# Softmax sums of an attention stage: three tiles of exponentials added on GpSimd ahead of the matmul, with the work around them moved between engines

## The chip, the core and the metric

One core of a Trainium2 chip runs the whole program. The metric is the device time of one execution in microseconds. Before the change three runs took 1913.70, 1917.08 and 1929.59 us; the median, 1917.08 us, is the time that counts.

## What is computed

The reference is one step of a model of two layers over 128 prompt tokens and 1024 sample tokens. Each layer projects its input for three groups of heads (a recurrence over a matrix state, attention with eight heads, a gated linear recurrence), multiplies each group by a gate, joins them in one output projection and normalises. The change lies in the attention and in the recurrence that is woven into its slots. Cut to that:

```python
s = (einsum('bqhd,bkhd->bhqk', qn, kn) + einsum('bqhr,bkr->bhqk', qr, kr)) * SOFTMAX_SCALE
p = softmax(s, axis=-1)                  # 1024 queries x 1152 keys, 8 heads
out = einsum('bhqk,bkhd->bqhd', p, v) * silu(gm)

# one step of the recurrence (per head and direction)
sa = einsum('ebhvk,ebhk->ebhv', S, -kk_t)
S = S * w_t + sa * (kk_t * a_t) + v_t * k_t
```

The kernel computes the recurrence in chunks of 64 tokens, for which a triangular matrix of each chunk is inverted: 16x16 blocks by substitution, the rest by matmuls.

## The kernel before, in words

The attention of a layer is cut into 16 units (8 heads x 2 blocks of 512 queries), and a unit into three slots: 48 slots a layer. In a slot the function `scores` (line 1126) is called for three tiles of 128 keys; each tile takes three matmuls (rounded and remainder parts) into one of three PSUM buffers `ps_a`, and ScalarE writes the exponentials into an SBUF tile `pe` (or `mxb`) of 128 keys x 512 queries. `values` (1138) then multiplies the three tiles with the values into `ps_pv`, and `sums` (1152) adds up the exponentials over the keys: for each tile and each quarter of the queries one matmul with 32 columns of the constant `two`, into `ps_rw`. Twelve such matmuls stand in a slot. With the unit's last tile VectorE takes the reciprocal of the sums into `rl`. `finish` (1176) spreads the reciprocals by a matmul and multiplies the unit's output `o` by them on VectorE; `gate` (1186) multiplies that by the gate on GpSimd and stores it. A softmax needs row maxima: `max_q`, `max_last` and `max_rows` (1096 to 1118) find them ahead of the unit, with VectorE reducing the PSUM buffer `ps_b`.

All other work of the stage is hung into the slots. The function `at` (1230) puts a call into one of six blocks of a slot; `run` calls them. The order within a slot is A0, scores, G, A1, B, values, C, sums, S (lines 1356 to 1367). On TensorE, VectorE and ScalarE the instructions keep exactly the order in which the program is written: the wrapper `in_line` (101) ties each to the one before it on its engine. GpSimd's instructions are not tied; a scheduler at build time orders them, by when it expects their operands. DMAs of the stage are issued by SyncE.

What else the change touches:

- `split_q` (1088): the queries are split into a rounded part (ScalarE) and a remainder `qo` (GpSimd, line 1092), in block G five slots ahead of the unit.
- The recurrence runs in nine windows a layer, one in four slots, around slot c: `win_products` (823) in block B of slots c-10 and c-9, with a mask on GpSimd (844); `inv_load` (863) in C of c-9 stores and loads the triangular blocks; `inv_blocks16` (874) in C of c-8 does the substitution: 15 steps of a product (881) and a sum (882) on GpSimd over 64 partitions, each step on the one before. `inv_store` (884) in A0 of c-5 copies the result on ScalarE and VectorE, stores and reloads it by DMA, and masks `Of` on GpSimd (895). `inv_blocks` (898) in G of c-4 masks the diagonal blocks, `BdT` on VectorE and `Bd` on GpSimd (900); `inv_product` (903) follows in block B of four slots.
- In block S stand `max_rows` (one in three slots, a matmul of shape 128x4) and, in the first layer, pieces of the next layer's conditioning (`adaln_piece`, matmuls of shape 128x32).

Of the kernel before, what the change touches and what calls it, by code (L numbers as in the profile page):

```python
# [10 lines left out]
F32 = mybir.dt.float32  # L11
# [44 lines left out]
def hybrid_kernel(ctx: ExitStack, tc: tile.TileContext, x_in, cT_in, kc_in, rope_in, vec_in,  # L56
# [270 lines left out]
    for l in range(layers):  # L327
# [342 lines left out]
        sums = P("pv")  # L670
# [152 lines left out]
        def win_products(i, s):  # L823

            w = wsets[i]
            ezr, abz, abr = w["ezr"], w["abz"], w["abr"]
            bkf = w["bk"].rearrange("p d f s z t -> p d f s (z t)")
            pk, pb = P("a"), P("a")
            pkv, pbv = (t.rearrange("p (d f c) -> p d f c", d=2, f=2) for t in (pk, pb))
            for d, f in units:  # L830
                for ps, o in ((pkv, 64), (pbv, 0)):
                    for eo in range(2):
                        rhs = ezr[half_(eo), eo, d, f, s].rearrange("p z t -> p (z t)")
                        mm(ps[half_(1 - eo if o else eo), d, f, :], lhsT=bkf[half_(eo), d, f, s, o:o + 64], rhs=rhs, start=True, stop=True)
            sca_.copy(abz[:, :, :, s], pbv[:, :, :, 0:64])
            sca_.copy(abr[:, :, s], pbv[:, :, :, 64:128])
            for eo in range(2):
                K_ = half_(1 - eo)
                vtt(ezr[K_, eo, :, :, s].rearrange("p d f z t -> p d f (z t)"), pkv[K_],
                    mask[K_, :, None, :].to_broadcast([64, 2, 2, 128]), op=MUL)  # L840
            if s == 1:
                for d in range(2):
                    v_ = abr[:, d].rearrange("p s f t -> p (s f) t")
                    gtt(v_, v_, mask[:, d, None, 64:128].to_broadcast([128, 4, 64]), op=MUL)

        def win_transposes(i):
            w = wsets[i]
# [26 lines left out]
        def inv_blocks16():  # L874
            vec_.tensor_copy(flat(U_)[32:64], flat(U_)[96:128, ::-1])
            nc.gpsimd.memset(X[0:64], 0.0)
            nc.gpsimd.memset(flat(X)[0:64, ::17], 1.0)
            for t in range(15, 0, -1):
                n = 16 - t
                tv = tmp[0:64, 0:t * n].rearrange("p (a b) -> p a b", a=t)  # L880
                gtt(tv, U_[0:64, 0:t, t:t + 1].to_broadcast([64, t, n]), X[0:64, t:t + 1, t:16].to_broadcast([64, t, n]), op=MUL)  # L881
                gtt(X[0:64, 0:t, t:16], X[0:64, 0:t, t:16], tv, op=ADD)  # L882

        def inv_store(i):
# [7 lines left out]
            for eo in range(2):  # L892
                dma(Bdc[64 * eo:64 * eo + 64], X_d[:, :, :, eo].rearrange("o d a i j -> i o (d a) j"))
            for d in range(2):
                gtt(Of[:, d].rearrange("p a (b c) -> p a b c", b=4), abz[:, d].rearrange("p f s (b c) -> p (f s) b c", b=4),
                    omask[:, d, None, :, None].to_broadcast([128, 4, 4, 16]), op=MUL)

        def inv_blocks():
            for o, t_, ttt in ((1, BdT, vtt), (0, Bd, gtt)):
                ttt(t_.rearrange("p d a (b j) -> p (d a) b j", b=4), Bdc[:, o, :, None, :].to_broadcast([128, 8, 4, 16]),  # L900
                    bmask[:, None, :, None].to_broadcast([128, 8, 4, 16]), op=MUL)

        def inv_product(i, n):
# [184 lines left out]
        def split_q(u):  # L1088
            qh, qo = u["qh"], u["qo"]
            ql = qo[0:96].bitcast(F32)  # L1090
            sca_.copy(qh[0:96], ql)
            gtt(qo[0:96], ql, qh[0:96], op=SUB)
            u["mx"], u["m1"] = T("sm", [128, 16]), T("sm", [128, 16])


        def max_q(u, qt):
# [52 lines left out]
                    u["o"] = W("ep", [128, 256])  # L1149
                    act(u["o"], u["pv"][:, 0:256], AF.Copy, scale=1 / 64)  # L1150

        def sums(u):

            end = NKS // 128 - 1 if u["q0"] < NS else 0
            for j, pe in u["pe"]:
                if j == 0:
                    u["sum"] = P("rw")
                for qt in range(4):
                    mm(u["sum"][32 * qt:32 * qt + 32, 0:128], lhsT=two[:, 0:32], rhs=pe[:, 128 * qt:128 * qt + 128],
                       start=j == 0, stop=j == end)  # L1160
                if j == end:
                    u["rl"] = W("ls", [128, 128])
                    vec_.reciprocal(u["rl"], u["sum"][:, 0:128])
            u["pe"] = []

        def load_gate(u):
            h, q0 = u["h"], u["q0"]
# [69 lines left out]
        for i, u in enumerate(us):  # L1237
# [2 lines left out]
                at(s0 - 6, "C", keys, u["h"])  # L1240
            at(s0 - 6, "A0", load_q, u)
            at(s0 - 5, "G", split_q, u)
            at(s0 - 4, "A1", max_q, u, 0)
            at(s0 - 3, "A0", max_q, u, 1)
            at(s0 - 3, "A1", max_q, u, 2)
# [2 lines left out]
            at(s0 - 2, "S", max_rows, u)  # L1248
            at(s0 + 2, "G", load_gate, u)
            if s0 + 4 < nslot:  # L1250
                at(s0 + 3, "C", finish, u)
                at(s0 + 4, "G", gate, u)
        for k_, todo_ in enumerate(ada_todo[2:]):
            ada_ = adaln_piece(*todo_)
            at(5 * k_ // 2 + 1, "S", next, ada_)
# [3 lines left out]
        for i in range(9):  # L1259
# [3 lines left out]
            at(c - 9, "B", win_products, i, 1)  # L1263
            at(c - 9, "C", inv_load, i)
            at(c - 8, "B", win_transposes, i)
            at(c - 8, "C", inv_blocks16)
            at(c - 5, "A0", inv_store, i)
            at(c - 4, "G", inv_blocks)
            for n in range(4):
# [36 lines left out]

        def prompt(u):
            values(u)
            sums(u)

        ups = [dict(h=4 * g, q0=NS, i=g, pe=[]) for g in range(2)]
        for u, t_ in zip(ups, (promptq[:, 0:2], promptq[:, 2:4])):
# [7 lines left out]
        for u in ups:  # L1320
            for t_ in u["qs"]:
                nc.gpsimd.memset(t_[96:128].bitcast(F32), 0.0)
            load_q(u)
            split_q(u)
            load_gate(u)
        ada_steps()
        early(-4)
# [25 lines left out]
        todo.setdefault((0, "C"), []).insert(0, (finish, (ups[1],)))  # L1353
        at(0, "S", gate, ups[1])
        line.update(on=True, last={})
        for slot in range(nslot):
            u = us[slot // 3]
            run(slot, "A0")
            for j in range(3):
                scores(u, 3 * (slot % 3) + j)  # L1360
            run(slot, "G")
            run(slot, "A1")
            run(slot, "B")
            values(u)
            run(slot, "C")
            sums(u)
            run(slot, "S")
        line["on"] = False
        out_y = {}

# [174 lines left out]
```

## Time and profile before

| what | us |
|---|---|
| runs: lowest, median, highest | 1913.70, 1917.08, 1929.59 |
| the profiled execution's own time | 1924.55 |
| its span, first to last instruction | 1922.6 |
| attention slots of layer 0 and of layer 1, in the span | 470 to 880, 1405 to 1812 |

The profile is of one execution, and durations below come from it. PE is TensorE's matmul, PEld its weight load, DVE is VectorE, ACT is ScalarE, POOL is GpSimd and SP is SyncE. A matmul of 32-bit numbers leaves two records. Matmuls are pipelined, so a record's duration is its latency, and neighbours overlap. "128*32" is the shape of the array that a matmul uses (rows*columns). L121 and L116 are lines of helpers through which all matmuls and all VectorE and ScalarE operations go, so groups are told apart by their tiles. What stands behind "<-" in brackets is what the engine waited for; "issue" is a gap for which the profile shows no other engine.

### The profile page before, as it was taken

Reading aid. Unit: us, or ns where it says so; the run is one execution under the profiler, and the core shown is the slowest. Engines: PE = TensorE matmul, PEld = TensorE weight load, DVE = VectorE, ACT = ScalarE, POOL = GpSimd, SP = SyncE. Lnnn points to the kernel's source line nnn. Section 1 sums busy time; section 2 is a strip of 40 time slices with the busy share of each in tenths; the row PEclk is TensorE's granted clock in tenths of the full one; section 3 lists DMA queues with packets and bytes.
Section 4 is the critical chain, followed back from the end, with each engine's and each line's share of the span. In section 5 each row is a group of like instructions: output and inputs, shape, how many; then the busy total and the mean of one; then the engine's idle time right before and its main releaser. Section 6 shows DMA issues by size and latency. Waiting matters only on the chain. (4 is left out here: it accounts for less than half of the span.)

```text
span 1922.6 us, 47689 instructions
## 1 busy us (share of the span) xinstructions
PE 1801.1 (94%) x18770; PEld 1513.2 (79%) x18770; DVE 1179.4 (61%) x2512; ACT 928.9 (48%) x2108; POOL 420.9 (22%) x916
## 2 busy tenths in 40 slices
PE   5898998989999999998999989999899999999798
PEld 3898887977787777766878989998767777777587
DVE  5744454784556655766777534558755566666676
ACT  2632565763444544554126326677544454455510
POOL 0010001042344434321011100101234344342100
PEclk7999998998999999998999999998999999999999
DMA  8335444674344444437443343436632333332642
GB/s 296 110 101 161 124 129 134 220 236 122 74 108 113 109 111 106 116 110 214 160 143 120 98 151 91 117 114 209 194 85 68 91 93 89 80 89 80 208 146 88
DMA packets 328896, 250.37 MB, mean 130 GB/s; under 512 B 105112, under 2 KB 268512, under 8 KB 327648
## 3 DMA queue, kind: packets, MB, share of 16 engines
q1 hardware_dynamic: 328672, 247.32, 43.6%
q8 instruction: 148, 2.42, 0.5%
q14 instruction: 76, 0.62, 0.1%
HBM read 168.55 MB, written 78.64 MB: 129 GB/s over the span
## 5 line engine op out<-in xcount | busy, mean ns | idle before, releaser
L121 PE MATMUL ps_a<-t,t 128*128 128x384 f32 (+4 forms) x6096 | 713.6, 296 | 35.8 <-ACT pe L116 13.8
L121 PEld LDWEIGHTS ps_a<-t,t 128*128 128x128 f32 (+1 forms) x6096 | 653.8, 167 | 70.9 <-ACT pe L116 21.9
L116 DVE TENSOR_REDUCE sm<-ps_b 128x1 f32<-128x1024 f32 (+1 forms) x164 | 179.8, 1096 | 124.7 <-PE ps_b L121 124.1
L116 ACT ACTIVATE pe<-ps_a 128x512 f32<-128x512 f32 (+1 forms) x296 | 168.5, 576 | 168.0 <-PE ps_a L121 155.4
L121 PE MATMUL ps_a<-q,t 128*128 128x512 f32 x864 | 223.5, 403 | 5.3 <-DVE ep L116 5.3
L121 PEld LDWEIGHTS ps_a<-q,t 128*128 128x128 f32 x864 | 161.4, 190 | 49.8 <-issue 7.3
L121 PE MATMUL ps_a<-t,q 128*128 128x512 f32 (+1 forms) x544 | 160.6, 379 | 0.0
L116 DVE TENSOR_TENSOR t<-kp,t 128x512 fp32r<-128x512 f32 (+2 forms) x128 | 83.2, 677 | 94.9 <-ACT t L116 85.5
L157 POOL TENSOR_TENSOR sm<-sm,nhalf 128x1 f32<-128x1 f32 (+1 forms) x54 | 40.5, 751 | 410.2 <-DVE sm L116 408.4
L121 PE MATMUL ps_pv<-pe,t 128*64 128x256 f32 x928 | 125.1, 391 | 0.0
L121 PE MATMUL ps_b<-t,q 96*128 96x512 f32 (+1 forms) x384 | 109.0, 378 | 13.5 <-DVE sm L116 8.4
L121 PE MATMUL ps_a<-t,kp 128*128 128x512 f32 (+1 forms) x304 | 116.3, 382 | 0.0
L121 PEld LDWEIGHTS ps_a<-t,q 128*128 128x128 f32 x544 | 99.8, 188 | 19.3
L116 ACT CAST t<-kp 128x512 fp32r<-128x512 f32 (+2 forms) x128 | 71.9, 602 | 86.9 <-DMA kp<-in_wft_dram 39.2
L121 PEld LDWEIGHTS ps_b<-t,q 96*128 96x128 f32 x384 | 63.1, 193 | 36.8 <-DVE sm L116 11.5
L121 PEld LDWEIGHTS ps_pv<-pe,t 128*64 128x64 f32 x928 | 60.0, 138 | 34.6 <-issue 8.0
L881 POOL TENSOR_TENSOR t<-t 64x15 f32<-64x15 f32 (+2 forms) x270 | 71.7, 265 | 62.1 <-DVE t L116 25.4
L882 POOL TENSOR_TENSOR t<-t 64x15 f32<-64x15 f32 (+2 forms) x270 | 73.1, 271 | 20.4
L116 DVE TENSOR_TENSOR t<-ps_a,t 128x512 f32<-128x512 f32 (+2 forms) x106 | 65.5, 625 | 17.5 <-ACT t L116 10.1
L121 PE MATMUL ps_rw<-pe,two 128*32 128x128 f32 x1888 | 75.7, 277 | 0.0
L121 PEld LDWEIGHTS ps_cx<-t,t 128*64 128x64 f32 (+1 forms) x1752 | 64.5, 138 | 13.9 <-issue 5.7
L116 ACT CAST q<-pe 128x512 fp32r<-128x512 f32 x32 | 19.9, 621 | 113.9 <-PE ps_a L121 102.0
(261 smaller groups left out, 2940.9 us busy)
## 6 DMA issues: line engine op xcount, KB each, us to landing
kp<-in_wft_dram SPq DMA_DIRECT2D x64, 256.0 KB
kp<-in_wmod_dram SPq DMA_DIRECT2D x64, 256.0 KB
rw<-in_x_dram SPq DMA_DIRECT2D x36, 256.0 KB
gate_d<-pe SPq DMA_DIRECT2D x48, 192.0 KB
bk_d<-ls SPq DMA_DIRECT2D x36, 256.0 KB
zr_d<-abz SPq DMA_DIRECT2D x36, 256.0 KB
t<-bk_d SPq DMA_DIRECT2D x18, 512.0 KB
t<-v_d SPq DMA_DIRECT2D x144, 64.0 KB
```

Of the source, the lines that this page charges most:

```text
L116: return lambda *a, **k: in_line(getattr(self.eng, op)(*a, **k))
L121: return in_line(nc.tensor.matmul(*a, **k))
L157: gtt(out, t[:, :n], nhalf.to_broadcast([128, n]), op=POW)
L881: gtt(tv, U_[0:64, 0:t, t:t + 1].to_broadcast([64, t, n]), X[0:64, t:t + 1, t:16].to_broadcast([64, t, n]), op=MUL)
L882: gtt(X[0:64, 0:t, t:16], X[0:64, 0:t, t:16], tv, op=ADD)
```

## The change

The three tiles of a slot are added up on GpSimd (`add_exps`) as their exponentials come, and four matmuls in place of twelve sum the result over the keys. They are issued one slot later, between block B and the values. The reciprocal becomes a function of its own (`invert`), after block C of the slot behind the unit's last one, and its result lies in `w2`, a tile of weights that is no longer needed there; `finish` and `gate` move one slot back. The remainder of the queries (`split_low`, block C), the mask of `win_products`, `Of` and `Bd` go from GpSimd to VectorE. The substitution becomes a generator of 16 pieces, spread over the blocks from C of slot c-8 to B of slot c-6.

```diff
-                    gtt(v_, v_, mask[:, d, None, 64:128].to_broadcast([128, 4, 64]), op=MUL)
+                    vtt(v_, v_, mask[:, d, None, 64:128].to_broadcast([128, 4, 64]), op=MUL)
...
             for t in range(15, 0, -1):
+                yield
                 n = 16 - t
...
-                gtt(Of[:, d].rearrange("p a (b c) -> p a b c", b=4), abz[:, d].rearrange("p f s (b c) -> p (f s) b c", b=4),
+                vtt(Of[:, d].rearrange("p a (b c) -> p a b c", b=4), abz[:, d].rearrange("p f s (b c) -> p (f s) b c", b=4),
...
-            for o, t_, ttt in ((1, BdT, vtt), (0, Bd, gtt)):
-                ttt(t_.rearrange("p d a (b j) -> p (d a) b j", b=4), Bdc[:, o, :, None, :].to_broadcast([128, 8, 4, 16]),
+            for o, t_ in ((1, BdT), (0, Bd)):
+                vtt(t_.rearrange("p d a (b j) -> p (d a) b j", b=4), Bdc[:, o, :, None, :].to_broadcast([128, 8, 4, 16]),
...
-            gtt(qo[0:96], ql, qh[0:96], op=SUB)
             u["mx"], u["m1"] = T("sm", [128, 16]), T("sm", [128, 16])
+
+        def split_low(u):
+            qo = u["qo"]
+            vtt(qo[0:96], qo[0:96].bitcast(F32), u["qh"][0:96], op=SUB)
...
-        def sums(u):
+        def sums(u, pe, first, last_):
             end = NKS // 128 - 1 if u["q0"] < NS else 0
-            for j, pe in u["pe"]:
-                if j == 0:
-                    u["sum"] = P("rw")
-                for qt in range(4):
-                    mm(u["sum"][32 * qt:32 * qt + 32, 0:128], lhsT=two[:, 0:32], rhs=pe[:, 128 * qt:128 * qt + 128],
-                       start=j == 0, stop=j == end)
-                if j == end:
-                    u["rl"] = W("ls", [128, 128])
-                    vec_.reciprocal(u["rl"], u["sum"][:, 0:128])
-            u["pe"] = []
+            if first == 0:
+                u["sum"] = P("rw")
+            for qt in range(4):
+                mm(u["sum"][32 * qt:32 * qt + 32, 0:128], lhsT=two[:, 0:32], rhs=pe[:, 128 * qt:128 * qt + 128],
+                   start=first == 0, stop=last_ == end)
+
+        def invert(u):
+            u["rl"] = w2[:, u["i"] % 2, 0:128]
+            vec_.reciprocal(u["rl"], u["sum"][:, 0:128])
+
+        def add_exps(u, n):
+            if n == 1:
+                u["acc"] = W("ls", [128, 512])
+                gtt(u["acc"], u["pe"][0][1], u["pe"][1][1], op=ADD)
+            else:
+                gtt(u["acc"], u["acc"], u["pe"][2][1], op=ADD)
...
+            at(s0 - 5, "C", split_low, u)
...
-                at(s0 + 3, "C", finish, u)
-                at(s0 + 4, "G", gate, u)
+                at(s0 + 4, "C", finish, u)
+                at(s0 + 5, "G", gate, u)
...
-            at(c - 8, "C", inv_blocks16)
+            sub_ = inv_blocks16()
+            for k_ in range(16):
+                k6 = 6 * (c - 8) + 4 + 3 * k_ // 4
+                at(k6 // 6, ("A0", "G", "A1", "B", "C", "S")[k6 % 6], next, sub_, None)
...
+        behind = None
         for slot in range(nslot):
             u = us[slot // 3]
             run(slot, "A0")
             for j in range(3):
                 scores(u, 3 * (slot % 3) + j)
+                if j:
+                    add_exps(u, j)
             run(slot, "G")
             run(slot, "A1")
             run(slot, "B")
+            if behind:
+                sums(*behind)
             values(u)
             run(slot, "C")
-            sums(u)
+            if slot % 3 == 0 and behind:
+                invert(behind[0])
+            behind = u, u.pop("acc"), u["pe"][0][0], u["pe"][-1][0]
+            u["pe"] = []
             run(slot, "S")
+        sums(*behind)
+        invert(us[-1])
```

## Rows read from the trace of the kernel before

**Rows 1.** Busy time by stage: us, busy (instructions) of each engine, clock, DMA share, GB/s.

```profile
core 0: us, PE busy (x) PEld busy (x) DVE busy (x) ACT busy (x) POOL busy (x), PEclk, DMA share, GB/s
...
470.00:880.00 410.00, 400.97 (x6489) 308.54 (x6488) 250.22 (x519) 204.04 (x451) 152.12 (x364) 0.98 0.42 111
...
1405.00:1812.00 407.00, 392.76 (x6254) 300.08 (x6252) 251.65 (x498) 208.56 (x460) 151.42 (x357) 0.99 0.38 97
```

**Rows 2.** Waits of weight loads, 470 to 880 us: total us, times, longest.

```profile
PEld ps_b L121 <- DVE sm L116: 4.8, 5, 3.4
...
PEld ps_pv L121 <- ACT pe L116: 1.8, 5, 0.7
```

**Rows 3.** Records with the tile `two`: count, ns least/median/most, first and last start.

```profile
L121 PE MATMUL ps_rw<-pe,two x1888: 272/273/423, 459.6 to 1805.8; 128*32 128x128 f32 x189
...
L121 PE MATMUL ps_rw<-mxb,two x448: 272/273/298, 490.4 to 1800.5; 128*32 128x128 f32 x150
```

**Rows 4.** Weight loads in time, 470 to 486 us: start, us, what, [idle before].

```profile
474.50 0.20 PEld L121 LDWEIGHTS ps_rw<-pe,two 128*32 128x32 f32 x8 [0.33 <-issue]
...
481.96 0.13 PEld L121 LDWEIGHTS ps_a<-ckvh,kp 128*64 128x64 f32 x1 [0.17 <-issue]
...
483.68 0.59 PEld L121 LDWEIGHTS ps_rw<-pe,two 128*32 128x32 f32 x24 [0.30 <-issue]
484.47 0.30 PEld L121 LDWEIGHTS ps_b<-t,q 96*128 96x128 f32 x2 [0.20 <-issue]
```

**Rows 5.** Weight loads in time, 538 to 550 us.

```profile
539.12 0.59 PEld L121 LDWEIGHTS ps_rw<-pe,two 128*32 128x32 f32 x24
539.72 0.20 PEld L121 LDWEIGHTS ps_b<-kc,sm 128*4 128x4 f32 x2
```

**Rows 6.** GpSimd's groups, 470 to 880 us: count, busy us, mean ns, idle before.

```profile
L1092 POOL TENSOR_TENSOR q<-q,q 96x512 fp32r<-96x512 f32 x14 | 17.8, 1269 | 27.9 <-ACT q L116 19.4 <-DVE modT L116 8.5
...
L844 POOL TENSOR_TENSOR t<-t,kc 128x256 f32<-128x256 f32 x16 | 11.4, 729 | 2.9 <-ACT t L116 2.9
L900 POOL TENSOR_TENSOR t<-t,kc 128x512 f32<-128x512 f32 x9 | 10.8, 1199 | 41.1 <-DMA t<-X_d 30.8 <-DVE rs L116 6.2 <-DVE ep L116 4.0
```

**Rows 7.** GpSimd in time, 608 to 630 us, one substitution from end to end.

```profile
614.80 0.73 POOL L1189 TENSOR_TENSOR ep<-ep,ep 128x256 f32<-128x256 f32 x1 [6.00 <-DVE ep L116]
616.27 0.21 POOL L881 TENSOR_TENSOR t<-t 64x15 f32<-64x15 f32 x1 [0.73 <-POOL ep L1189]
...
628.45 0.21 POOL L882 TENSOR_TENSOR t<-t 64x15 f32<-64x15 f32 x1
```

**Rows 8.** All engines in time, 629 to 642 us.

```profile
631.14 1.02 ACT L116 COPY t<-t 32x256 f32<-32x256 f32 x2
633.53 0.60 ACT L116 ACTIVATE mxb<-ps_a 128x512 f32<-128x512 f32 x1 [1.37 <-PE ps_a L121]
...
635.31 0.54 PEld L121 LDWEIGHTS ps_a<-t,t 64*64 64x64 f32 x16 [0.36 <-issue]
```

**Rows 9.** All engines in time, 518.9 to 523 us.

```profile
519.04 0.21 POOL L882 TENSOR_TENSOR t<-t 64x15 f32<-64x15 f32 x1
...
520.19 1.04 ACT L116 COPY t<-t 32x256 f32<-32x256 f32 x2
521.91 0.60 ACT L116 ACTIVATE pe<-ps_a 128x512 f32<-128x512 f32 x1 [0.68 <-PE ps_a L121]
```

**Rows 10.** VectorE's groups, whole run: count, busy us, mean ns, idle before.

```profile
L116 DVE TENSOR_TENSOR kp<-pe,q 128x512 fp32r<-128x512 f32 x32 | 22.5, 703 | 8.1 <-PE ps_a L121 6.1 <-ACT q L116 1.9
...
L116 DVE TENSOR_TENSOR st<-st,wcs 128x256 f32<-128x256 f32 x36 | 16.3, 454 | 1.2
...
L116 DVE TENSOR_TENSOR t<-t,kc 128x512 f32<-128x512 f32 x18 | 13.5, 749 | 8.3 <-DMA t<-X_d 8.3
```

**Rows 11.** All engines in time, 789 to 793 us.

```profile
789.84 1.52 POOL L900 TENSOR_TENSOR t<-t,kc 128x512 f32<-128x512 f32 x1 [4.06 <-DMA t<-X_d]
790.38 1.26 DVE L116 TENSOR_TENSOR rw<-rw,rw 128x256 f32<-128x256 f32 x1
```

More of the change, by code (lines that the diff above doesn't have):

```diff
@@ L1308, in prompt @@
             values(u)
-            sums(u)
+            sums(u, u["pe"][0][1], 0, 0)
+            invert(u)
+            u["pe"] = []
         ups = [dict(h=4 * g, q0=NS, i=g, pe=[]) for g in range(2)]
@@ L1324, in hybrid_kernel @@
             split_q(u)
+            split_low(u)
             load_gate(u)
@@ L1363, in hybrid_kernel @@
             run(slot, "B")
+            if behind:
+                sums(*behind)
             values(u)
             run(slot, "C")
-            sums(u)
+            if slot % 3 == 0 and behind:
+                invert(behind[0])
+            behind = u, u.pop("acc"), u["pe"][0][0], u["pe"][-1][0]
+            u["pe"] = []
             run(slot, "S")
+        sums(*behind)
+        invert(us[-1])
         line["on"] = False
```

## The prediction

> **What bounds the kernel now.** I read the busy time by stage first, then who waits for whom in the attention stage, then the order of TensorE's weight loads, and last GpSimd. The change touches only the attention slots, 48 a layer, which fill 470 to 880 us and 1405 to 1812 us: about 8.5 us a slot. There TensorE is busy 401 of 410 us and 393 of 407, VectorE 250, ScalarE 204 to 209, GpSimd 152 [rows 1]; the clock is granted almost in full. TensorE's queue hardly waits for another engine: its weight loads stood 4.8 us in the whole first stage for VectorE's row maxima and 1.8 us for an exponential [rows 2]. So a record taken from TensorE here shortens the slot, and time added elsewhere costs only where TensorE comes to wait for it.
>
> **TensorE: fewer sums.** Each of a slot's 12 sums matmuls leaves two records; the run has 1888 + 448 = 2336 of them [rows 3], which is 2 x (96 slots x 12 + 16 of the prompt). Adding the three tiles first leaves 4 matmuls, 8 records. What is one worth? Not the 0.27 us that each lasts, since four column groups run side by side. The weight loads tell: a group of 8 takes 0.20 us, a group of 24 takes 0.59 [rows 4], so 16 records cost 0.39 us. 96 slots x 0.39 = 37.4 us, the main term. From above: two thirds of everything between the group's start at 483.68 and the next load at 484.47, 0.53 us a slot or 51 us; from below nothing, if another engine becomes late.
>
> **TensorE: the sums at another place.** They stood between block C and block S; now they stand between B and the values. A change of the array's shape leaves gaps: 0.20 us from the sums' 128x32 to 96x128, 0.17 from 32x64 to 128x64 [rows 4]. Most slots swap one such change for another: taken as nothing, with 0.2 us either way. But in some 45 of the 96 slots block S holds work of the same or a like narrow shape (30 times the maxima's transposition, 16 times the conditioning matmuls), which today follows the sums with no gap: loads end at 539.71, the next starts at 539.72 [rows 5]. There the sums now need a change of their own, about 0.2 us: +9 us, bounds 0 and +19. The Trainium skill speaks against the move as well: "TensorEngine Tiling (Array Packing)", section Tiling Modes, Key Properties, says that a change of tiling mode, not of tile, drains the engine. The gaps of [rows 4] agree with that.
>
> In return the values, which wait for the third exponential, have the sums in front of them, and the sums' operand is a slot old: of the 1.8 us a layer waited there [rows 2] I take back 2 us in both layers.
>
> **GpSimd.** It gets two additions of 128x512 a slot. The trace shows none; the nearest is the split's subtraction of 96x512 with two full operands, 1.27 us [rows 6]. I take 1.27 (bounds 1.2, the masked 512 columns there with a broadcast operand, and 1.5). 96 additions a layer are 122 us; the split, the masks and the diagonal blocks leave (17.8 + 11.4 + 10.8 = 40 us [rows 6], plus the off-diagonal mask). GpSimd goes from 152 to about 230 of 400 us: enough room on average. An addition ends a few us behind its exponential, and its sum is due in block B of the next slot, 8 us on, so the new wait should cost TensorE nothing; if it does, the values and all that follows on TensorE stand behind it (rival four). The exponentials' buffers now also wait for the additions, with several us to spare.
>
> The tight place is the substitution. Behind its result stand, in program order, ScalarE's and VectorE's copies in block A0 three slots later, and behind those on ScalarE the exponentials of that slot. Today it runs from 616.27 to 628.66 [rows 7]; ScalarE's copies take 1.02 us and the next exponential starts at 633.53 [rows 8], so the result could come until 632.5, 3.9 us later, without harm. In a tight case the result comes at 519.25, copies at 520.19, the exponential at 521.91 [rows 9]: 1.6 us to spare. Now four additions (5.1 us) and, in two of three cases, a gate of 0.73 us fall into this stretch, and a split of 1.27 us leaves it: about 4.5 us later. Reading all 18 windows in this way, seven have under 5 us to spare, the others up to 10. TensorE itself can bear about 1 us more: the exponential of 633.53 ends at 634.13 and block B, which needs its buffer, begins at 635.31 [rows 8]. So seven windows lose on average some 0.9 us: +6 us, bounds 0 and 18 x 2 = 36 us. Spreading the substitution itself removes no instruction; it lets the additions in between. I price it at nothing else.
>
> **VectorE.** A window hands it four products of 128x256 at 0.454 us and one of 128x512 at 0.749; each of 18 groups of queries in a layer, one subtraction of 96x512, 0.703 at most [rows 10]. 9 x (4 x 0.454 + 0.749) + 18 x 0.703 = 36 us a layer: 250 becomes 286 of some 400 us. It waits mostly for TensorE, so this hides, at the price of a few longer waits for row maxima: +3 us, bounds 0 and +10. The subtraction now waits on VectorE for ScalarE's copy of the block before; with chain and maxima queued behind it, that copy must not be late, and its operand was loaded a slot earlier.
>
> **VectorE against GpSimd.** At 789.84 GpSimd's masked product takes 1.52 us, and VectorE's 128x256 addition behind it at 790.38 takes 1.26 instead of about 0.45 [rows 10, 11]: the two hold each other up. In the +3 above stand some 3 such VectorE operations a slot, a third of which meet an addition and lose about 0.4 us, all beside TensorE. "SBUF — State Buffer", section "SBUF: two separate sides", of the Trainium skill states this as a rule: a VectorE operation with two SBUF inputs and a GpSimd operation that reads SBUF exclude each other, and the later one fully blocks. By it rival two, below, would come; the trace agrees in the row shown.
>
> The finish and the gate come one slot later and the reciprocal follows the next slot's block C: nothing waits for them but the store of a head's output, which is read after the stage; at the stage's end the last addition hides behind the last values, within 1 us. DMAs are the same in number; the gate's two stores move past the loads of one slot on SyncE's queue, which has room.
>
> **The sum.** -37.4 + 9 - 2 + 6 + 3 = -21.4 us. The profiled execution took 1924.55 us, so 1903.1. The runs' median is 1917.08, 7.5 us below it: 1895.7, said as 1896.
>
> **Rivals.** *One: GpSimd's lateness eats the gain.* If every window's substitution is 2 us late for TensorE, 36 us go in place of the 6 I took: -21.4 + 30 = +8.6, about 1926; at half of it -21.4 + 12 = -9.4, 1908. Either is no change that can be measured. For it: 12.4 us of substitution and four additions in two slots of 8.2. Against: the other two slots of a window are light.
> *Two, the slower side: the shared access makes VectorE the bound.* Should each of its three two-input operations a slot be blocked as at 790.38, by 0.8 us, VectorE needs (250 + 36) / 48 = 6.0 plus 2.4 = 8.4 us a slot. It decides from the point where VectorE's slot passes TensorE's 8.1; with its in-order waits for TensorE on top, say 8.8 us, the slots cost 96 x 0.3 = 29 us more than today: 1946. Against: GpSimd's subtractions of 1.27 us keep a mean of 1.269 [rows 6], so clashes are rare.
> *Three: more comes back.* The full 0.53 us a slot and no dearer changes of shape: -51 + 6 = -45, 1872.
> *Four: the sums wait for the addition after all,* if GpSimd's queue puts it behind other work by over a slot: 0.3 us a slot gives 29 us back, 1925, no change.
>
> **How the numbers follow.** A measurement of this kernel tells about 1% from no change, 19 us. My forecast has 0.48, centred on 1896, with its own range 1884 to 1908: 0.39 of it faster by over 1%, 0.09 within. Rival one 0.24 (0.21 within, 0.03 slower), two 0.11 (0.09 slower, 0.02 within), three 0.10 (faster), four 0.07 (0.06 within, 0.01 slower). Faster 0.49, the same 0.38, slower 0.13. The range goes from just above rival three to the near edge of rivals one and four: 1874 to 1922.
>
> **What would show it.** Right: 800 records of the sums instead of 2336; groups of 8 at 0.20 us; both stages shorter by some 10 us, slots near 8.3 us; additions near 1.27 us, GpSimd busy about 230 us a stage; no waits of TensorE for GpSimd. Wrong: weight loads for the sums released by GpSimd (rival four); ScalarE's copies of the substitution waiting for GpSimd in most windows (one); VectorE's SBUF products at twice their time, with row maxima late (two); gaps of 0.3 us and more on both sides of the sums (the second term mis-sized).

## The result, and the profile after

The changed kernel is slower: 1949.17 us median (1939.02 to 1951.89) beside 1921.31 us (1913.70 to 1929.59) of the kernel before in the same session, ratio 1.0134 [1.0106, 1.0161]. The forecast was 1896, its range ended at 1922. The profiled execution took 1951.04 us, its span 1949.2.

The busy time of the two attention stages, which answers to [rows 1] (us, busy time and instructions of each engine, granted clock, DMA share, GB/s):

```profile
470.00:880.00 410.00, 387.38 (x5695) 285.62 (x5694) 290.18 (x565) 197.35 (x439) 225.34 (x404) 0.97 0.41 105
...
1405.00:1812.00 407.00, 376.60 (x5374) 277.19 (x5369) 275.33 (x518) 193.47 (x436) 219.72 (x407) 0.96 0.33 83
```

TensorE does less and is less busy, 387 of 410 us in place of 401; VectorE (290) and GpSimd (225) have what the forecast gave them (286 and 230). Nobody is full, and yet the same work no longer fits: from the first score of slot 0 to that of slot 47, layer 0 takes 409.6 us in place of 402.7, layer 1 412.8 in place of 390.5. The clock fell with TensorE's pauses: 0.97 for 0.98 and 0.96 for 0.99, which is 4 + 12 us of full-speed time.

The sums' records (count, ns least/median/most, first and last start) answer to [rows 3], the weight loads in time to [rows 4]:

```profile
L121 PE MATMUL ps_rw<-ls,two x768: 269/297/423, 489.6 to 1835.7; 128*32 128x128 f32 x192
...
L121 PE MATMUL ps_rw<-pe,two x32: 272/359/423, 461.1 to 1415.3; 128*32 128x128 f32 x32
```

```profile
543.11 0.16 PEld L121 LDWEIGHTS ps_rw<-ls,two 128*32 128x32 f32 x8
543.47 0.20 PEld L121 LDWEIGHTS ps_pv<-mxb,t 128*64 128x64 f32 x4 [0.20 <-issue]
```

So the change does what it says: 800 records for 2336, a group of 8 in 0.16 us, a 0.20 us gap for the change of shape behind it.

What TensorE waits for: weight loads, 470 to 885 us, beside [rows 2], and then matmuls, 1405 to 1840 us (total us, times, longest):

```profile
PEld ps_b L121 <- DVE sm L116: 12.2, 14, 3.5
...
PEld ps_a L121 <- DVE ys L116: 7.9, 4, 2.8
...
PEld ps_rw L121 <- POOL ls L1173: 2.2, 4, 1.7
```

```profile
PE ps_b L121 <- DVE sm L116: 9.2, 10, 3.2
PE ps_a L121 <- DVE ys L116: 8.8, 4, 2.6
PE ps_a L121 <- DMA t<-zr_d: 7.7, 4, 3.4
```

The wait for VectorE's row maxima was 4.8 us and is 12.2. That for VectorE's addition to `ys` is 7.9; before the change, in the same stretch, it was

```profile
PEld ps_a L121 <- DVE ys L116: 0.9, 2, 0.5
```

Four waits of 2.2 us in all are for an addition: the sums hardly wait for GpSimd. In layer 1 there is a third kind, for the window's loads.

How VectorE comes to be late is seen in slot 10 of layer 0 (all engines in time; start, us, engine, operation, [idle before]):

```profile
557.50 1.27 POOL L1173 TENSOR_TENSOR ls<-pe,pe 128x512 f32<-128x512 f32 x1 [2.27 <-ACT pe L116]
557.54 1.77 DVE L116 COPY t<-t 32x256 f32<-32x256 f32 x2
...
559.34 1.90 DVE L116 TENSOR_TENSOR t<-abz,kc 128x256 f32<-128x256 f32 x2
...
559.70 1.25 POOL L1175 TENSOR_TENSOR ls<-ls,pe 128x512 f32<-128x512 f32 x1
...
561.95 0.41 DVE L116 TENSOR_TENSOR ys<-ps_a,ys 128x256 f32<-128x256 f32 x1
...
562.42 1.50 PE L121 MATMUL ps_a<-t,t 64*64 64x128 f32 x28 [2.60 <-DVE ys L116]
```

Two copies take 1.77 us (0.69 before), because one of them ends only after the addition of 557.50 has; two products, work moved to VectorE, take 1.90 (0.84 alone), because one ends only after the addition of 559.70 has. Behind them on VectorE stands the addition to `ys` that frees TensorE's PSUM buffer, and TensorE stands 2.60 us for it. Before the change these matmuls waited for nothing, and the slot took 8.6 us; now it takes 13.8.

### The profile page after: what moved, and what is told of

Its sections match the earlier page's. It is cut to its first block, busy times and chain, and to the rows that moved or that the text cites. A ratio compares the mean times of both kernels' runs of the same rounds, so it can differ in the third digit from the quotient of the medians.

```text
span 1949.2 us, 44758 instructions
## 1 busy us (share of the span) xinstructions
PE 1787.8 (92%) x17234; PEld 1474.2 (76%) x17234; DVE 1268.7 (65%) x2638; ACT 926.9 (48%) x2108; POOL 557.6 (29%) x982
## 5 line engine op out<-in xcount | busy, mean ns | idle before, releaser
L121 PE MATMUL ps_a<-t,t 128*128 128x384 f32 (+4 forms) x6096 | 717.7, 298 | 67.7 <-DVE ys L116 15.8
L121 PE MATMUL ps_a<-q,t 128*128 128x512 f32 x864 | 229.8, 409 | 9.1 <-ACT pe L116 6.7
L121 PE MATMUL ps_pv<-pe,t 128*64 128x256 f32 x928 | 130.8, 405 | 0.0
L1173 POOL TENSOR_TENSOR ls<-pe,pe 128x512 f32<-128x512 f32 x58 | 76.1, 1313 | 116.7 <-ACT pe L116 113.9
L1175 POOL TENSOR_TENSOR ls<-ls,pe 128x512 f32<-128x512 f32 x78 | 100.3, 1285 | 3.4 <-ACT pe L116 0.7
L883 POOL TENSOR_TENSOR t<-t 64x15 f32<-64x15 f32 (+2 forms) x270 | 75.3, 279 | 18.6
```

The costliest lines, as they stand in the source:

```text
L121: return in_line(nc.tensor.matmul(*a, **k))
L1173: gtt(u["acc"], u["pe"][0][1], u["pe"][1][1], op=ADD)
L1175: gtt(u["acc"], u["acc"], u["pe"][2][1], op=ADD)
```

## The experiments

Theory one: GpSimd's additions and VectorE's SBUF operations hold each other up, and VectorE, which works in order, frees TensorE's buffers late. Theory two: the additions make GpSimd late, and what stands behind GpSimd (the copies of the substitution, the gate's store on SyncE's queue) makes TensorE late. In the first four expectations theory three lays the loss to the work moved to VectorE, and theory four to the sums' new place. "Slot lengths" below run from a slot's first score to the next slot's.

**e1_no_adds: the changed kernel without additions.**

```
-                u["acc"] = W("ls", [128, 512])
-                gtt(u["acc"], u["pe"][0][1], u["pe"][1][1], op=ADD)
-            else:
-                gtt(u["acc"], u["acc"], u["pe"][2][1], op=ADD)
+                u["acc"] = val(0)
```

> The changed kernel without the additions on GpSimd: the four sums matmuls of a slot read a tile of values that is long finished, so the softmax is divided by something else. Theory 1 (the additions and VectorE's operations on SBUF shut each other out, TensorE then waits for VectorE, and the clock halves behind such waits): all of that goes, ratio to the kernel before 0.983 to 0.990, about 1890 to 1902 us. Theory 2 (GpSimd's queue is too full, so the substitution's result and the gate's store come late): the same ratio, as that queue empties too. Theory 3 (the work moved to VectorE is too much for it by itself): the loss stays, ratio 1.005 or more, 1930 us or more. Theory 4 (the sums at their new place cost TensorE what they save): 0.997 to 1.003.

1896.80 us, ratio 0.9846 [0.9800, 0.9893]. The additions alone cost what lies between this and 1949: 52 us. All else in the change together gains 28 us. Theories one and two had forecast the same here, so this run does not tell them apart; the causes that theories three and four name do not explain the loss.

**e2_sums_alone: in addition the four moved operations back on GpSimd and the substitution in one piece.** The diff is that of e1 and the change's own, reversed.

> As the run without additions, and besides masks, off-diagonal and diagonal blocks and the low part back on GpSimd and the substitution in one piece: only the 4 matmuls a slot later are left of the change (on a finished tile, so the softmax is divided by something else). Theories 1, 2 and 3: ratio 0.980 to 0.990, my main term of 37 us less some 10 for changes of shape. Theory 4: 0.997 to 1.003. Against the run without additions it tells what the moved work costs where no addition stands in its way: theory 1 within 0.004, theory 3 at least 0.015 below.

1910.12 us, ratio 0.9907 [0.9874, 0.9939]: the four matmuls a slot later are worth 15 us by the medians and 18 by the ratio, less than the 30 of the first three terms of the sum. The moved work and the spread substitution, which e1 has and this run has not, are worth 13 us more: where no addition stands in its way the moved work gains. Two rows of the weight loads' waits tell part of what the 30 us lacked, 470 to 885 us, and below them the second one before the change:

```profile
PEld ps_b L121 <- DVE sm L116: 10.6, 14, 3.0
...
PEld ps_pv L121 <- issue: 9.7, 48, 0.4
```

```profile
PEld ps_pv L121 <- issue: 3.7, 19, 0.4
```

TensorE, now earlier, meets VectorE's row maxima more often: 14 waits of 10.6 us for 5 of 4.8 [rows 2], and 12.1 us for 8.4 in layer 1, 9.5 us in both. And the gap for the change of shape stands before the values of every slot (48 times, 9.7 us, where it was 19 times, 3.7). All gaps of that kind, on all tiles, grow by 7.4 us in layer 0 and, without its longest one, 6.7 in layer 1. Besides, slot 29 of layer 1 is 6.6 us longer than before, for a reason that e6 shows.

**e3_adds_vector: the changed kernel with additions on VectorE, and the other parts undone as in e2.**

```
-                gtt(u["acc"], u["pe"][0][1], u["pe"][1][1], op=ADD)
+                vtt(u["acc"], u["pe"][0][1], u["pe"][1][1], op=ADD)
-                gtt(u["acc"], u["acc"], u["pe"][2][1], op=ADD)
+                vtt(u["acc"], u["acc"], u["pe"][2][1], op=ADD)
```

> The two additions of a slot on VectorE instead of GpSimd; masks, blocks, low part and the substitution in one piece back on GpSimd as before. VectorE gets 96 x 0.69 = 66 us a stage more, GpSimd nothing. Theory 1: no additions hold GpSimd's side of the access, so most of the gain appears, ratio 0.985 to 0.997. Theory 2: the same, GpSimd's queue is as before. Theory 3 (VectorE has no room in the stage): slower, ratio 1.01 or more. Theory 4: 1.00 or more.

2014.92 us, ratio 1.0458 [1.0406, 1.0510]: far off for theories one and two, on the side of theory three (1.01 or more). TensorE's waits, 1405 to 1840 us:

```profile
PE ps_a L121 <- DVE t L116: 13.3, 9, 1.9
PE ps_a L121 <- DVE ys L116: 12.8, 8, 2.0
PE ps_b L121 <- DVE sm L116: 11.0, 11, 3.5
```

VectorE, busy 282 of 407 us, has no room for them: what counts is what stands in front of the operation that frees a buffer, not the sum of busy time. This is theory one's second half, shown without any addition on GpSimd.

**e4_moves_only: the kernel before, with masks, blocks, products and low parts on VectorE.**

```
-                gtt(v_, v_, mask[:, d, None, 64:128] ... op=MUL)
+                vtt(v_, v_, mask[:, d, None, 64:128] ... op=MUL)
...
-            gtt(qo[0:96], ql, qh[0:96], op=SUB)
...
+            at(s0 - 5, "C", split_low, u)
```

> The kernel before with nothing but the mask, the off-diagonal and diagonal blocks and the low part moved to VectorE (36 us a stage). Theories 1, 2 and 4: within 0.995 to 1.004. Theory 3: ratio 1.015 or more, for then the moved work alone makes the loss.

1912.01 us, ratio 0.9935 [0.9910, 0.9960]: better than both kernels, and just under the 0.995 at which the expectation of theories one, two and four ended. The forecast had put +3 us on this part. Where its slots gain is narrow: slot 12 of each layer, 13.2 to 10.3 us and 16.1 to 10.9, where the kernel before waits for row maxima and loses its clock (0.80 from 1505 to 1522 us); the other slots keep their length within 0.7 us, but for slot 0 of layer 0 (-1.6) and slot 44 of layer 1 (+2.3).

**e5_fill: in place of each addition one of 8 columns and two fills, together about as long, that read hardly anything.**

```
-                gtt(u["acc"], u["acc"], u["pe"][2][1], op=ADD)
+                gtt(u["acc"][:, 0:8], u["acc"][:, 0:8], u["pe"][2][1][:, 0:8], op=ADD)
+            for _ in range(2):
+                nc.gpsimd.memset(u["acc"][:, 8:512], 0.25)
```

and likewise for the first addition of a slot.

> The changed kernel, with GpSimd's additions cut to 8 columns (they wait for the same exponentials) and, behind each, two fills of the other 504 columns of the same array: GpSimd is kept busy at the same points, about as long, and reads hardly anything from SBUF. The sums over keys are those of the fill. Theory one, the additions lengthen VectorE's operations through SBUF (in the changed kernel the sum of two halves in the group norm takes 0.69 us in the mean against 0.42 without additions, the window's second product 0.73 against 0.42): with little read, that is gone, near the run without additions, 1895 to 1910 us, ratio 0.984 to 0.992, and these two operations near 0.42 us. Theory two, the additions make what stands behind them on GpSimd late (the substitution, the gate's product and its store on SyncE's queue): no difference from the changed kernel, 1940 to 1955 us, ratio 1.008 to 1.016.

1905.25 us, ratio 0.9889 [0.9846, 0.9932]. The stages of this run, and then VectorE's groups in it and in the changed kernel (whole run; count, busy us, mean ns, idle before; the group of `rw` mixes shapes in both):

```profile
470.00:880.00 410.00, 392.66 (x5780) 288.32 (x5779) 279.12 (x588) 207.58 (x461) 222.34 (x602) 0.98 0.44 116
1405.00:1812.00 407.00, 384.27 (x5480) 283.78 (x5479) 277.78 (x564) 207.62 (x459) 215.19 (x579) 0.98 0.39 100
```

```profile
L116 DVE TENSOR_TENSOR rw<-rw,rw 128x256 f32<-128x256 f32 (+2 forms) x56 | 24.8, 442 | 14.4 <-ACT rw L116 14.1
...
L116 DVE TENSOR_TENSOR t<-abz,kc 128x256 f32<-128x256 f32 x36 | 13.7, 423 | 0.6
...
L116 DVE TENSOR_TENSOR sm<-sm 128x4 f32<-128x4 f32 x32 | 5.4, 170 | 1.1
L116 DVE TENSOR_SCALAR smr<-gmv 128x4 f32<-128x4 f32 x18 | 4.8, 268 | 0.6
```

```profile
L116 DVE TENSOR_TENSOR rw<-rw,rw 128x256 f32<-128x256 f32 (+2 forms) x56 | 33.8, 604 | 14.7 <-ACT rw L116 14.5
L116 DVE TENSOR_TENSOR t<-abz,kc 128x256 f32<-128x256 f32 x36 | 24.9, 732 | 0.6
...
L116 DVE TENSOR_SCALAR smr<-gmv 128x4 f32<-128x4 f32 x18 | 10.5, 581 | 0.6
L116 DVE TENSOR_TENSOR sm<-sm 128x4 f32<-128x4 f32 x32 | 9.8, 307 | 1.1
```

GpSimd is as busy as in the changed kernel (222 and 215 us for 225 and 220), if not quite as late: a substitution takes 12.7 us in the mean from its first operation to its last, 14.6 in the changed kernel, 10.9 in e1. VectorE's products and additions are back at their length (25 window products that met a fill took 0.422 us in the mean), and 44 of the 52 us are back with them. TensorE's waits for VectorE in the slots fall from 39.8 us to 18.4, about as in e1 (table behind the experiments). This settles the greater part for theory one. Of the remaining 8 us, to e1, 5.6 stand in one slot, 34 of layer 0:

```profile
771.31 1.03 ACT L116 COPY t<-t 32x256 f32<-32x256 f32 x2 [6.38 <-POOL t L883]
773.02 0.09 PEld L121 LDWEIGHTS ps_a<-ep,kc 128*2 128x2 f32 x2 [3.61 <-ACT pe L116]
```

ScalarE's copies wait for the substitution there, and TensorE for an exponential behind them: GpSimd's lateness by itself. The two runs' intervals overlap.

**e6_gate_vector: the changed kernel with the gate's product on VectorE.**

```
-            gtt(gm, gm, u["o"], op=MUL)
+            vtt(gm, gm, u["o"], op=MUL)
```

> The changed kernel, with the gate's product on VectorE instead of GpSimd, nothing else. Theory two: the gate's stores no longer wait on SyncE's queue behind GpSimd's additions, the window's loads behind them come in time, and the two slots of layer 1 that are 6.8 and 6.4 us longer than before lose that: 1930 to 1940 us, ratio 1.003 to 1.009. Theory one: 1945 to 1952 us, ratio 1.011 to 1.016, one more VectorE operation for each third slot and nothing else.

1944.82 us, ratio 1.0090 [1.0061, 1.0120], between the two forecasts and hardly apart from the changed kernel's. But the two slots named are back: slots 17 and 29 of layer 1, 15.0 and 14.6 us in the changed kernel for 8.2 before, are 8.1 again. In the profiled execution the slots of both layers are 19 us shorter than in the changed kernel, but the stretch between the two layers' slots is 10 us longer. That stretch takes 526 to 539 us in the profiled executions, so a few us between totals say little of the slots. What happens in the two slots named is seen in slot 17 of the changed kernel (GpSimd, SyncE's queue, then TensorE):

```profile
1557.54 0.74 POOL L1200 TENSOR_TENSOR ep<-ep,ep 128x256 f32<-128x256 f32 x1
```

```profile
1553.45 0.38 SPq L994 DMA_DIRECT2D yr_d<-ys  x1
1558.30 1.24 SPq L1204 DMA_DIRECT2D yT_d<-ep  x2
1559.63 1.28 SPq L816 DMA_DIRECT2D t<-zr_d  x2
```

```profile
1563.44 0.66 PE L121 MATMUL ps_a<-t,t 64*64 64x128 f32 x2 [3.38 <-DMA t<-zr_d]
```

The gate's store (L1204) waits on SyncE's queue for GpSimd's late gate (L1200), and the window's loads (L816) behind it come 3.4 us late for TensorE. It does not need the additions: in e1, e2 and e5 slot 29 of layer 1 is 6.1, 6.6 and 5.9 us longer than before too. TensorE's clock then fell; the stretch around it (granted clock in the third column from the right):

```profile
1530.00:1563.00 33.00, 29.19 (x492) 22.44 (x490) 22.50 (x47) 17.58 (x41) 19.89 (x42) 1.00 0.36 90
1563.00:1570.00 7.00, 6.12 (x62) 3.91 (x64) 1.38 (x2) 0.75 (x3) 2.03 (x2) 0.51 0.28 70
1570.00:1600.00 30.00, 26.96 (x428) 19.80 (x426) 23.04 (x38) 14.10 (x31) 12.49 (x21) 1.00 0.26 63
```

After a pause of 3.4 us TensorE works some 7 us at 1.2 instead of 2.4 GHz: the wait costs about as much again.

**e7_one_piece: the changed kernel with the substitution unspread.**

```
-                k6 = 6 * (c - 8) + 4 + 3 * k_ // 4
+                k6 = 6 * (c - 8) + 4
```

> The changed kernel, with the substitution in one piece again, as before. Theory one: it costs little by itself, 1945 to 1955 us, ratio 1.010 to 1.017. Theory two: a run of about 10 us on GpSimd ahead of the next slot's additions makes the sums wait, TensorE stands, 1955 to 1975 us, ratio 1.017 to 1.027; against that, the substitution ends a slot earlier, and if its end is what is late for the copies on VectorE and ScalarE, 1925 to 1940 us, ratio 1.000 to 1.009.

1949.91 us, ratio 1.0117 [1.0068, 1.0166]: as theory one said. These runs tell no cost and no gain of the spreading.

**e8_half_slots: additions in slots 0 and 3 of each four only.**

```
-                if j:
+                if j and slot % 4 in (0, 3):
                     add_exps(u, j)
...
-            behind = u, u.pop("acc"), u["pe"][0][0], u["pe"][-1][0]
+            if "acc" in u:
+                behind = u, u.pop("acc"), u["pe"][0][0], u["pe"][-1][0]
+            else:
+                behind = None
+                for j, pe in u["pe"]:
+                    sums(u, pe, j, j)
+                if slot % 3 == 2:
+                    invert(u)
```

> The changed kernel, with additions and late sums only in slots 0 and 3 of each four; in slots 1 and 2 the three tiles' sums are taken from the exponentials in the same slot, 12 matmuls, as before. The slots that the change lengthened most are 2 of each four (18.7 us in each layer) and 1 of layer 1 (8.4 us). Theory one (clash in the slots where VectorE's operations of the window stand): these 46 us go and 48 slots give back 8 records of 24 ns each, 9 us: 1905 to 1918 us, ratio 0.990 to 0.997. Theory two (lateness, which gathers in slots 3 and 0 where the substitution runs): half the additions stand beside the substitution as before, half the loss stays: 1922 to 1940 us, ratio 0.999 to 1.009.

1939.45 us, ratio 1.0083 [1.0058, 1.0108]: a miss for theory one as put. The expectation gave 9 us for the sums of the 48 slots; but 8 matmuls more in a slot are 16 records, so it is 768 records, and at the 24.6 ns of [rows 4] (0.59 us for 24) 19 us. TensorE's waits, 470 to 885 us, name a wait that the edit itself brought, the reciprocal that still reads the one PSUM buffer of the sums:

```profile
PE ps_rw L121 <- DVE w L116: 10.1, 4, 4.0
```

**e12_half_early: the same with the reciprocal ahead of the values.**

```
                 sums(*behind)
+                if slot % 3 == 0:
+                    invert(behind[0])
             values(u)
             run(slot, "C")
-            if slot % 3 == 0 and behind:
-                invert(behind[0])
```

> The run with additions in slots 0 and 3 of each four, with one edit: the reciprocal of the finished sums comes right behind the last late sums, ahead of the values, instead of after the values. In the run before, 20.7 us of TensorE's waits (10.1 and 10.6 us in the two stages, 4 each) were for that reciprocal: the next sums were written to the same PSUM buffer in the same slot. Theory one: these waits go, the time comes where the first expectation had put it: 1915 to 1926 us, ratio 0.995 to 1.000. Rival (half of the additions still hold VectorE up half as much, and the waits only change their name): 1932 to 1940 us, ratio 1.004 to 1.008.

1926.82 us, ratio 1.0019 [1.0002, 1.0035], one us above theory one's range, which would end 10 us higher with 19 us for the sums (the run has 1568 records of them, the changed kernel 800). e1 plus 19 us is 1916, so the additions that are left cost some 11 us. In each stage TensorE still waits once for the reciprocal, which the edit brought; the row reads the same in both:

```profile
PE ps_rw L121 <- DVE w L116: 3.6, 1, 3.6
```

In slots 2 of each four, which have no additions here, TensorE's matmuls wait 3.6 us in both layers together: 4.4 before the change, 32.7 in the changed kernel. So most of the loss was gathered there, as the expectation of e8 had it, and additions in slots 0 and 3 cost little.

**e9_adds_alone: the changed kernel with masks, blocks, products and low parts back on GpSimd and the substitution in one piece; the additions stay.** The diff is the change's own, reversed, but for additions and sums.

> The changed kernel with its three other parts undone: masks, blocks and low parts on GpSimd again where they were, substitution in one piece; additions on GpSimd and the late sums stay. Theory one: of the 52 us by which VectorE's operations beside additions are longer in the changed kernel, 11.1 are the window's second product, 1.7 the low parts of q and about half of 3.4 the blocks, so some 14 us of 52 are no longer VectorE's; that share of the 53 us that the additions cost comes back, about 15 us, against which GpSimd has 45 us a stage more in front of its additions and late work: 1935 to 1946 us, ratio 1.005 to 1.011. Rival: what counts is how late GpSimd runs, and 45 us more a stage make it worse: 1955 to 1975 us, ratio 1.016 to 1.027.

1942.77 us, ratio 1.0081 [1.0049, 1.0114], in theory one's range, but only in part by its reason. TensorE's waits for VectorE are 10 us less than in the changed kernel; those for ScalarE, behind a substitution that now takes 16.5 us, are 7 us more; and slots 17 and 29 of layer 1, where the window's loads came late, are 13 us shorter together. Beside e2 the additions cost 33 us here, beside e1 they cost 52. Of this difference (25 us in the slots' lengths) 14 lie in the same two slots, so that additions are dearer the more VectorE has to do through SBUF is shown for 11 us at most.

**e10_c5_aside: the changed kernel with the copies of the inverse on ScalarE and the window's two products on GpSimd.**

```
-            vec_.tensor_copy(flat(XO)[32:64], flat(X)[32:64, ::-1])
+            sca_.copy(flat(XO)[32:64], flat(X)[32:64, ::-1])
...
-                vtt(Of[:, d].rearrange( ...
+                gtt(Of[:, d].rearrange( ...
```

> The changed kernel, with the four VectorE operations of the window's slot c-5 taken off VectorE: the two copies of the inverse on ScalarE, the two products of the window on GpSimd. Theory one, in its narrow form: these stand in line ahead of the addition that frees TensorE's buffer in that slot, and of the 18.7 us that the slots 2 of each four are longer in each layer nearly all goes: 1918 to 1932 us, ratio 0.997 to 1.004. Theory one, in its wide form, any lengthened operation of VectorE makes the next buffer late, wherever it stands: these four carry 15 of 52 us, so 15 of 53 come back: 1931 to 1940 us, ratio 1.004 to 1.008. Rival: the slots are long because of GpSimd's work itself; with two more operations there, 1950 to 1960 us, ratio 1.013 to 1.018.

1934.29 us, ratio 1.0046 [1.0023, 1.0070]: in the range of the wide form, but not for its reason. Slots 17 and 29 of layer 1 are 14 us shorter together than in the changed kernel, because the wait for the window's loads is gone; the slots of both layers together are 11 us shorter. Slots 2 of each four are as long as in the changed kernel (19 and 21 us more than before), and what TensorE waits for there has changed. Its waits for VectorE's `ys`, 15.8 us in the changed kernel, are gone, as the narrow form had it; those for exponentials are 26.0 us for 8.0. Slot 34 of layer 0:

```profile
780.30 2.07 ACT L116 COPY t<-t 32x256 f32<-32x256 f32 x4 [5.33 <-POOL t L883]
782.39 1.08 ACT L116 ACTIVATE pe<-ps_a 128x512 f32<-128x512 f32 x2
783.04 0.09 PEld L121 LDWEIGHTS ps_a<-ep,kc 128*2 128x2 f32 x2 [2.61 <-ACT pe L116]
```

Four copies on ScalarE wait for the substitution, the exponentials behind them, and TensorE for these: rival one of the prediction, met here.

**e11_one_operand: the fills of e5 as operations with one operand.**

```
-                nc.gpsimd.memset(u["acc"][:, 8:512], 0.25)
+                nc.gpsimd.tensor_scalar(u["acc"][:, 8:512], u["pe"][j][1][:, 8:512], 1.0, None, op0=ADD)
```

> As the run with fills, but each fill is an operation that reads one operand, the exponentials of one tile, and adds 1 (504 columns); again two behind each addition of 8 columns, and the sums over keys are those of such an array. If VectorE is held up only beside operations with two operands from SBUF: as the run with fills, 1898 to 1910 us, ratio 0.986 to 0.992. If any reading holds it up: as the changed kernel, 1938 to 1955 us, ratio 1.007 to 1.016. In proportion to what is read, in between.

2082.51 us, ratio 1.0817 [1.0783, 1.0852], outside every forecast, and so no answer by its time: the operation lasts 1.48 us where two operands took 1.27. GpSimd's group, 470 to 885 us:

```profile
L1177 POOL TENSOR_SCALAR ls<-pe 128x504 f32<-128x504 f32 x128 | 189.7, 1483 | 24.9 <-ACT pe L116 22.9
```

GpSimd is then busy 339 of 415 us, and the exponentials wait for their buffers. VectorE's operations give part of an answer. Those that met nothing but this operation lengthen, but less than beside an addition: the masks of diagonal blocks, 128x512, take 0.88 us in the mean of 19 and at most 1.10 (0.68 alone; at most 1.77 beside an addition), products of 128x256 0.46 in the mean of 30 and at most 0.82 (0.41 alone). The run also shows lateness as a cost of its own, at some 6 us of added work a slot; at 2.5 us (e5) there was little of it.

**TensorE's waits in the slots, by run.** The table sums the idle time before TensorE's matmuls from slot 0 to slot 47 of both layers, by the engine that ended it, in one profiled execution each. "Clock" is the time that the granted clock lacked to full speed there, "slots" the length of both stretches (all in us).

| run | VectorE | ScalarE | DMA | clock | slots |
|---|---|---|---|---|---|
| before | 15.3 | 1.1 | 1.0 | 6.8 | 793 |
| changed kernel | 39.8 | 9.7 | 7.7 | 25.5 | 822 |
| e1, no additions | 18.6 | 1.5 | 4.8 | 5.1 | 769 |
| e5, fills | 18.4 | 5.8 | 4.6 | 11.9 | 778 |
| e9, additions alone | 29.9 | 16.4 | 0.6 | 13.7 | 801 |
| e10, c-5 aside | 24.1 | 28.5 | 0.1 | 21.5 | 812 |
| e12, half, early | 21.3 | 3.4 | 0.5 | 6.8 | 789 |

## Why the prediction was wrong

**What held.** The records, the gap, the additions' duration (1.27 to 1.33 us), both engines' busy time, and that the sums would not wait for GpSimd (rival four) came as said. 50 of 94 slots are shorter, most of them by 0.2 to 1.1 us.

**The step that failed: "VectorE against GpSimd".** The size of the clash was in the text: 3 operations a slot, a third of them meeting an addition, 0.4 us each, which is 38 us in 96 slots. Over both stages of the changed kernel 106 VectorE operations beside an addition are, in sum, 52 us longer than the median of the same operation without one: about 0.5 us each. (That this sum is as large as what the additions cost is chance: TensorE loses what stands behind such an operation, and the clock besides.) What was wrong are the words "all beside TensorE", and with them the +3 us. VectorE works in order, and behind a held operation stands, soon, one that TensorE waits for: a row maximum, or an addition that frees a buffer. e5 gives 44 us for this term in place of 3; in the slots, by the table, they are 21 us of waits for VectorE, 4 for ScalarE, 3 for loads, and 14 that the lower clock cost. That GpSimd's subtractions kept a mean of 1.269 in the kernel before was no evidence: it is VectorE's operations that lengthen, and the additions are many more.

**Rival two** had this mechanism and a near time, 1946, at 0.11, but the wrong point from which it decides. It asked when VectorE's sum of work passes TensorE's slot; VectorE is at 290 of 410 us and no bound. In-order waits decide, long before that point. e3 shows the same without GpSimd: additions on VectorE cost 105 us beside e2 at a busy time that would have fitted. The Trainium skill's rule in "SBUF — State Buffer", section "SBUF: two separate sides", that the later of the two is blocked for the whole instruction, was quoted and then priced at a third. The runs agree with it for the window's product: beside an addition the window's product rises from 0.424 to at most 1.569 us, that is by 1.15, nearly the whole 1.27; beside fills, which read nothing, it stays at 0.423.

**Smaller steps.** The saved matmuls and their new place, -37.4 + 9 - 2 = -30 us, measured -15 by the medians, -18 by the ratio (e2). The main term was misread: the group of 8 in [rows 4] stood in a stretch at half the clock (0.50, third column from the right):

```profile
468.00:475.00 7.00, 6.95 (x40) 5.13 (x39) 2.41 (x4) 1.56 (x3) 4.78 (x16) 0.50 0.19 44
```

At full clock a group of 8 takes 0.16 us, as in the changed kernel, so 16 records are worth 0.43 us and 96 slots 41. Against that, the changes of shape cost 14 us in place of 9, inside their bounds, and the sum lacked two waits: 9.5 us in which TensorE, being earlier, stands for VectorE's row maxima, and 6.6 us in slot 29 of layer 1. The moved work, +3 for VectorE's share, measured -13 alone (e4), a gain; the two medians' differences, -15 and -13, make up e1's -28, though part of each is the same wait in slot 12. The substitution's lateness, +6, was about right: TensorE waits 9.7 us for ScalarE in the changed kernel, 1.1 before, and ScalarE's copies wait for the substitution in 8 of 18 windows, where the prediction had seven that lose. Spreading it is worth nothing that shows (e7), as priced. "SyncE's queue, which has room" was wrong in layer 1: there the late store held the window's loads, at 6 to 7 us in a slot.

**The account**, in medians: 1921 to 1925 before, 1897 with all parts but the additions, 1905 with GpSimd as busy but not reading, 1949 with the additions. What would be kept is e4, 1912 us: the moves without additions.

**Left open.** How much of the loss an addition with one operand would bring: e11 shows only that VectorE's operations lengthen less beside one. Whether additions in slots 0 and 3 alone, without the wait for the reciprocal, would gain beside e4 was not run. Of e4's 13 us 6 lie in the slots in the profiled executions (8 gained in slot 12, some lost elsewhere); another 6 lie between the two layers' slots, where executions differ by as much.

## What to carry to other kernels

An engine with room in its busy time can still be the bound when it works in order: price an added or lengthened operation by what stands behind it, up to the first instruction that frees a buffer or releases a semaphore of the bounding engine. Before giving GpSimd work on SBUF, list VectorE's operations that read and write SBUF alone and count those that it will meet, at up to the whole length of GpSimd's operation; running the same GpSimd time as fills tells access from lateness in one run. And a step that is moved takes its DMAs along: look at what is queued behind them.

## What the runs showed of the hardware that was not expected

Tiny operations are held almost as long as large ones: VectorE's 128x4 TENSOR_SCALAR `smr<-gmv` rose from 0.170 to 1.012 us beside an addition. Operations that read PSUM are not touched: `t<-ps_a,t` took 0.685 us in the mean beside additions, 0.677 in the median without, the row maxima of 128x512 0.685 and 0.676. The batch-norm statistics, 0.210 us alone, kept 0.212. Beside fills, which read nothing, some operations with one operand lengthen, where products of two operands do not: in e5 nine copies of 32x256 that met a fill took 0.52 us in the mean (0.31 alone), five of `smr<-gmv` 0.37 (0.17 alone). And GpSimd's operation with one operand and a constant took longer, 1.48 us for 504 columns, than its addition of two operands of 512.
